# Giving GpSimd's work to VectorE and ScalarE, and keeping silu(cond) in DRAM, in a two-layer fp32 diffusion backbone

## The chip, the cores and the metric

The kernel runs on one core of a Trainium2 chip. The metric is the device time of one execution in microseconds (us), the median over runs. The core has five engines that matter here: TensorE (PE in the profile; PEld is its weight load), VectorE (DVE), ScalarE (ACT), GpSimd (POOL) and SyncE (SP), whose queue issues nearly all DMAs. Each engine works through its own instructions in order and waits on semaphores for the others.

## The reference

Two trunk layers over 512 latent and 128 context tokens of width 1024, all in fp32. The part that matters:

```python
def trunk_layer(x, cond, layer_idx, p, rope_mla, rope_diff, ctx):
    mod = jax.nn.silu(cond) @ p['ada_w'] + p['ada_b']
    shift, scale, gate = jnp.split(mod, 3, axis=-1)
    h = rmsnorm(x, p['norm_g']) * (1.0 + scale) + shift
    parts = jnp.split(h @ p['w_in'], _split_offsets(), axis=-1)
    c_q, c_kv, k_rope, cb, cc, cx, dq, dk, dv, z = parts
    ...
    o_mla, ckv, kr = mla_branch(c_q, c_kv, k_rope, p['q_norm'], p['w_uq'], p['kv_norm'], p['w_ukv'],
                                rope_mla, ctx_mla)
    o_conv = conv_branch(cb, cc, cx, p['conv_w'])
    ...
    o_diff, k_d, v_d = diff_branch(dq, dk, dv, p['lam'], p['subln'], lambda_init, rope_diff, ctx_diff)
    mix = jnp.concatenate([o_mla, o_conv, o_diff], axis=-1) * jax.nn.silu(z)
    x = x + gate * (mix @ p['w_out'])
    return x, (ckv, kr, k_d, v_d)
```

The latent attention (`mla_branch`) and the differential attention (`diff_branch`, two softmax maps a head) have four heads each; `k_rope` is rotated by `rope_mla` before it is used as a key. `cond` is one vector of 1024 for the latent tokens and one for the context tokens, so `mod` of a layer is 2 x 3072 numbers from a 1024 x 3072 matrix `ada_w`. A last RMSNorm closes the trunk. The outputs are both token groups and the new keys and values of each layer.

## The kernel before

x lies transposed in SBUF: 128 partitions, 8 blocks (`kt`) of the model width, 640 tokens. The tokens are worked on in two halves of 320 (`j` = 0, 1). Every fp32 product is done as three matmuls on split operands: `mm3` multiplies high by high (L362), high by low (L363) and low by high (L364). So every weight is loaded raw over the SP queue (L319), ScalarE casts it to its high part (`whi_...`, L324), and the low part `wli_... = raw - high` is one subtraction (L326) on the engine that the unit was given: GpSimd for the units qk2, cq1, c01, c11 of both layers and qk0, dv0 of layer 2, VectorE for the rest. A weight unit is 15 + 4 per layer, each in two halves of about 512 KB; the raw and split tiles come from a pool of 11 buffers with the tag "w".

The start: the condition vectors `cond` are loaded, silu is taken by ScalarE (L122, tanh) and VectorE (L123, L124) into `sc`, and 32 loads of 256 KB of the first layer's adaLN matrix (`ada`, L441) alternate on the SP queue with the loads of x (L416). Part 0 is summed by VectorE, parts 1 to 3 by TensorE (`pa`, L462), then moved and completed on VectorE (`mod`, L470, L161). Meanwhile the squares of x half 0 are taken by ScalarE (L236) and added up by GpSimd (L245), `st_n` and `rb_n` on TensorE turn the sum into a scale, VectorE forms `t` (L373), and `modulate` makes the high and low part of h: `hh` on ScalarE (L390), `hl` on VectorE (L394). The first projection `p0qk` runs over half 0 while GpSimd squares half 1 (L238, all eight issued at `kt` = 1 of that loop), VectorE adds them up, and the second half follows.

After that a generator `main()` emits all input projections of a layer, `units()` the attention units of both kinds (scores `S`/`Sm`, row maximum `sm`/`smm` on VectorE, exponential `E`/`Em` on ScalarE, transposes `tpd`/`tpm`, products `O`/`Om`), a list `bg` holds the work behind a projection (rotations, norms, weight splits), and `side()` computes the remaining adaLN vectors (the gate of layer 1 and all of layer 2) piece by piece on VectorE. `side()` needs silu(cond) broadcast over the partitions: `silu_bcast` loads 512 numbers of each of the two raw vectors to all partitions into the one buffer `cb` (L136), takes tanh on ScalarE into `tb` (L140, a tile of the "w" pool), and finishes silu with two VectorE instructions (L141, L142). It does so four times. Then for each piece `at` of 128 x 512 weights (L148, 256 KB) two multiply-and-sum instructions `jk` (L153) follow on VectorE. The rotary key of the latent attention is rotated by `rope` (L545, L547, L551 on GpSimd for `krf`, on VectorE for the other calls).

A scheduler of the tile framework sets the order of each engine's instructions from its own estimate of when they become ready, except where `pin` keeps program order (the first loads and casts, and the `cb` loads). So work given to another engine is placed anew, and the order around it shifts too.

Of the kernel before, what the change touches and what calls it, by code (L numbers as in the profile page):

```python
# [60 lines left out]
def tile_kernel(ctx: ExitStack, tc: tile.TileContext, i: dict, o: dict):  # L61
    nc = tc.nc
    V, S, G, TE = nc.vector, nc.scalar, nc.gpsimd, nc.tensor

# [8 lines left out]
    NBLK, NW = 37, 11  # L73
    PU = ("qk2", "cq1", "c01", "c11")
    QD, QM = 5, 3
# [48 lines left out]
    V.tensor_tensor(out=sc, in0=th0, in1=cond, op=ALU.mult)  # L124


    mod = [[cst.tile([P, KT, 2], F32, name="mod%d_%d" % (l, s)) for s in range(3)] for l in range(DEPTH)]
# [5 lines left out]

    def silu_bcast(hf, name):
        for c in range(2):
            pin(nc.sync.dma_start(out=cb2[:, c, :],  # L136
                                  in_=i["cond2"][c:c + 1, hf * 512:(hf + 1) * 512].broadcast_to([P, 512])))
        tb = wp.tile([P, 1024], F32, tag="w", name="tb" + name, bufs=NW, padded_shape=[P, 1088])
        tb = tb.rearrange("p (c n) -> p c n", c=2)
        S.activation(tb, cb2, AF.Tanh, scale=0.5)  # L140
        V.tensor_scalar(out=tb, in0=tb, scalar1=0.5, scalar2=0.5, op0=ALU.mult, op1=ALU.add)  # L141
        V.tensor_tensor(out=cb2, in0=cb2, in1=tb, op=ALU.mult)  # L142

# [80 lines left out]
    class Norm:  # L224


        def __init__(self, j, name, tag="blk", eng=V, sq=S):
            self.sq = sq
            self.j, self.name, self.sqs, self.tag, self.eng = j, "%s%d" % (name, j), [], tag, eng

        def add(self, x, kt):
            nm = "sq%s%d" % (self.name, kt)
            sq = slot(nm, shape=(P, HB)) if self.tag == "blk" else vtile(nm)[:, 0:HB]
            xj = x[:, self.j * HB:(self.j + 1) * HB]
            if self.sq is S:
                S.activation(sq, xj, AF.Square)  # L236
            else:
                self.sq.tensor_tensor(out=sq, in0=xj, in1=xj, op=ALU.mult)  # L238
            self.sqs.append(sq)
            while len(self.sqs) > (1 if kt == KT - 1 else 2):  # L240
                self.merge()

        def merge(self):
            a, b = self.sqs[0:2]
            self.eng.tensor_tensor(out=a, in0=a, in1=b, op=ALU.add)  # L245
            del self.sqs[1]
# [64 lines left out]

    def load_unit(src, w, name, tags, eng, res):

# [7 lines left out]
        for hf in range(2):  # L321
            hi = wtile_new(w, "wh%s%d" % (name, hf), tags[hf], F32R)
            lo = wtile_new(w, "wl%s%d" % (name, hf), tags[hf], F32R)
            pin(S.copy(hi, raws[hf]), len(loaded) < 4)  # L324
            yield
            eng.tensor_tensor(out=lo, in0=raws[hf], in1=hi.bitcast(F32), op=ALU.subtract)  # L326
            res.append((hi, lo))
            yield

    for l in range(DEPTH):  # L330
        for u in range(NU):
            src = i["wi"][l, :, :, 4 * UOFF[u]:4 * UOFF[u + 1]].rearrange("h p (k c) -> h p k c", k=4)
            unit_q.append((src, UW[u], "i%d_%s" % (l, UNITS[u]), ("w", "w"), G if l > 0 and u < 2 or UNITS[u] in PU else V))
        for u in range(4):
            unit_q.append((i["wo"][l, u].rearrange("h p (k c) -> h p k c", k=4), 256, "o%d_%d" % (l, u),
                           ("w", "w") if u < 3 else ("qs", "kh"), V))
    loaded = []
# [73 lines left out]
    x_dram = dr.tile([P, KT, T], F32, name="x_dram")  # L411
    norms = [Norm(0, "n0", "v", G), Norm(1, "n0", sq=G)]

# [97 lines left out]
    for l in range(DEPTH):  # L511
# [27 lines left out]

        def rope(dst, src, cos, sin, mask, name, rs=slice(0, P), eng=V):  # L540

            sh = slot("sh" + name, shape=(P, NL))
            V.stream_shuffle(sh[rs], lat(src)[rs], mask)
            yield
            eng.tensor_tensor(out=lat(dst)[rs], in0=lat(src)[rs], in1=cos[rs], op=ALU.mult)  # L545
            yield
            eng.tensor_tensor(out=sh[rs], in0=sh[rs], in1=sin[rs], op=ALU.mult)  # L547
            yield
            if eng is G:
                yield  # L550
            eng.tensor_tensor(out=lat(dst)[rs], in0=lat(dst)[rs], in1=sh[rs], op=ALU.add)  # L551
            yield
# [203 lines left out]
        def kv_post(krt, ck):  # L756
# [11 lines left out]
            S.activation(sq, ck, AF.Square)  # L768
            yield from rope(krf, kr, cosm, sinm, SWAP8, "kr%d" % l, rs, G)
            ckA = slot("ckA%d" % l)  # L770
# [190 lines left out]
        def main():  # L961
# [4 lines left out]
            for j in range(2):  # L966
                ps = [bank("p%dqk0%d%d" % (l, b, j))[:, 0:HB] for b in range(2)]
                js = slice(j * HB, (j + 1) * HB)
                for kt in range(KT):
# [12 lines left out]
                    if l == 0 and j == 0:  # L982
                        if kt == 1:
                            for k in range(KT):
                                norms[1].add(xs[k], k)
                        if kt == 6:
                            rg = norms[1].rstd()
# [38 lines left out]
        def side():  # L1026

            for step, (hf, parts) in enumerate((((0, ((l, 2),)), (1, ((l, 2), (l + 1, 0), (l + 1, 1))),
                                                 (0, ((l + 1, 0), (l + 1, 1))))) if l + 1 < DEPTH else
                                               ((0, ((l, 2),)), (1, ((l, 2),)))):  # L1030
                if step > 0 or l == 0:
                    silu_bcast(hf, "%d%d" % (l, step))
                for ll, s in parts:
# [194 lines left out]
def _layout(inp):  # L1228
# [6 lines left out]
    r["cond"] = np.stack([a["c"][0].reshape(P, KT), a["c_ctx"].reshape(P, KT)], axis=-1)  # L1235
    r["cond2"] = np.stack([a["c"][0], a["c_ctx"]])
    r["ident"] = np.concatenate([np.eye(P), np.zeros((P, 2))], axis=1).astype(np.float32)
# [84 lines left out]
```

## Time and profile before

| | |
|---|---|
| median of 3 runs (lowest, highest) | 825.05 us (823.18, 825.55) |
| the profiled execution: its time, its span | 825.69 us, 823.9 us |
| mean granted TensorE clock | 0.989 |
| busy: PE, PEld, DVE, ACT, POOL | 785.5, 741.3, 622.1, 449.9, 68.9 us |
| chain that ended last, shares | PE 70%, DVE 13%, DMA 7%, ACT 5%, issue 3%, POOL 1% |
| HBM read, written | 78.14 MB, 6.46 MB |

The span is the time from the first to the last instruction of the profiled execution; 1.8 us of its time lie outside it. Busy times say how full an engine is on the average; what ends a wait has to be read from the chain and the waits of one stretch. A granted clock of 1.00 is 2.4 GHz on TensorE, 0.50 is 1.2 GHz.

### The profile page before, as it was taken

The page shows a single profiled execution, that of the slowest core. Times are in us where ns is not written, and L with a number is a line of the kernel's source. Part 1 is how long each engine was busy: PE and PEld are TensorE (multiplying, and loading weights), DVE is VectorE, ACT ScalarE, POOL GpSimd, SP SyncE. Part 2 cuts the span into 40 slices and gives each one's busy share as a digit, 9 for nine tenths or more (in the row PEclk, how much of TensorE's full clock was granted, in tenths as well). Part 3 has the DMA queues.
Part 4 walks back from the last instruction along what each step waited for, and adds up shares of the span by engine and source line. Part 5 has one row for each costly group of instructions (what it writes and reads, how often), then busy time and mean ns, then how long its engine had stood idle before and what let it go on. Part 6 is the DMA issues. An engine that isn't in the chain of part 4 may idle for free.

```text
span 823.9 us, 14193 instructions
## 1 busy us (share of the span) xinstructions
PE 785.5 (95%) x5390; PEld 741.3 (90%) x5390; DVE 622.1 (76%) x1414; ACT 449.9 (55%) x978; POOL 68.9 (8%) x45
## 2 busy tenths in 40 slices
PE   6999998999999988999999999999999899999994
PEld 1389998999999988999999999999999899899994
DVE  4788998989897677779567478877788556668635
ACT  2255456556666566673334556565667567755310
POOL 3300020030002002000220001011000200200000
PEclk9999999999999999999999999999999999999997
DMA  8926424221421232135730322222212201221503
GB/s 309 386 74 187 144 69 158 75 88 57 146 84 39 55 132 88 46 122 188 246 103 27 100 82 68 64 64 71 93 39 77 65 26 65 64 91 43 189 1 127
DMA packets 66163, 85.51 MB, mean 104 GB/s; under 512 B 4976, under 2 KB 47408, under 8 KB 66096
## 3 DMA queue, kind: packets, MB, share of 16 engines
q1 hardware_dynamic: 65520, 83.96, 31.2%
q8 instruction: 42, 0.69, 0.3%
q10 hardware_dynamic: 576, 0.66, 0.2%
q14 instruction: 25, 0.20, 0.1%
HBM read 78.14 MB, written 6.46 MB: 103 GB/s over the span
## 4 chain that ended last, share of the span: by engine, by line
PE 70%; DVE 13%; DMA 7%; ACT 5%; issue 3%; POOL 1%; SPq 0%; POOLq 0%; DVEq 0%; ACTq 0%
PE wo L363 4%; PE wo L364 4%; PE wo L362 4%; PE O L651 3%; DVE jk L153 2%; PE v L362 2%; PE v L364 2%; PE v L363 2%; PE S L620 2%; PE p1qk L363 2%; PE p1qk L362 2%; PE tpm L905 2%; PE p1qk L364 2%; PE p1c L362 2%; PE p1c L363 2%
## 5 line engine op out<-in xcount | busy, mean ns | idle before, releaser
L153 DVE CUSTOM_DVE_ANT_0 jk<-at,cb 128x512 bf16<-128x512 f32 x128 | 89.6, 700 | 8.7 <-DMA at<-in_adaT 7.7
L637 ACT ACTIVATE E<-S,sm 128x640 f32<-128x640 f32 (+1 forms) x80 | 56.5, 709 | 45.5 <-DVE sm L631 41.7
L363 PE MATMUL wo<-mx,who 128*128 128x320 f32 x256 | 78.9, 311 | 0.5 <-DVE mx L274 0.2
L364 PE MATMUL wo<-mx,wlo 128*128 128x320 f32 x256 | 78.5, 309 | 0.0
L362 PE MATMUL wo<-mx,who 128*128 128x320 f32 x256 | 78.2, 311 | 0.0
L631 DVE TENSOR_REDUCE sm<-S 128x1 f32<-128x640 f32 (+1 forms) x80 | 55.0, 711 | 5.4 <-PE S L621 5.0
L236 ACT ACTIVATE sqn<-xn 128x320 f32<-128x320 f32 x32 | 14.9, 470 | 64.2 <-DVE xn L1170 57.5
L894 ACT ACTIVATE Em<-Sm,smm 128x640 f32<-128x640 f32 (+1 forms) x40 | 28.3, 708 | 39.0 <-DVE smm L892 37.7
L363 PEld LDWEIGHTS wo<-mx,who 128*128 128x128 f32 x256 | 48.0, 188 | 1.4 <-DVE mx L274 1.3
L364 PEld LDWEIGHTS wo<-mx,wlo 128*128 128x128 f32 x256 | 48.1, 188 | 0.0
L362 PEld LDWEIGHTS wo<-mx,who 128*128 128x128 f32 x256 | 47.7, 188 | 0.0
L362 PE MATMUL v<-whi_dv,hh 128*128 128x272 f32 x160 | 46.3, 290 | 0.0
L363 PE MATMUL v<-wli_dv,hh 128*128 128x272 f32 x160 | 46.0, 288 | 0.0
L364 PE MATMUL v<-whi_dv,hl 128*128 128x272 f32 x160 | 46.0, 288 | 0.0
L620 PE MATMUL S<-kh,qs 128*128 128x320 f32 x128 | 40.6, 327 | 5.4 <-ACT E L637 4.6
L651 PE MATMUL O<-v,atd 128*128 128x128 f32 x336 | 43.9, 274 | 0.0
L363 PE MATMUL p0qk<-hl,whi_qk 128*128 128x320 f32 x128 | 40.0, 313 | 2.4 <-DVE hl L394 2.4
L326 POOL TENSOR_TENSOR wli_c<-ri_c,whi_c 128x1024 fp32r<-128x1024 f32 x8 | 19.8, 2477 | 267.9 <-PE p1zm L363 84.9
L651 PEld LDWEIGHTS O<-v,atd 128*128 128x128 f32 x336 | 41.9, 191 | 0.0
L362 PE MATMUL p1c<-hh,whi_c 128*128 128x320 f32 x128 | 41.5, 325 | 0.0
L362 PE MATMUL p0c<-hh,whi_c 128*128 128x320 f32 x128 | 41.5, 324 | 0.0
L362 PE MATMUL p0qk<-hh,whi_qk 128*128 128x320 f32 x128 | 39.6, 320 | 1.4 <-ACT hh L390 1.4
(375 smaller groups left out, 2627.7 us busy)
## 6 DMA issues: line engine op xcount, KB each, us to landing
at<-in_adaT SPq DMA_DIRECT2D x64, 256.0 KB, 3.9
ada<-in_adaA SPq DMA_DIRECT2D x32, 256.0 KB, 5.1
ri_qk<-in_wi SPq DMA_DIRECT2D x16, 512.0 KB, 4.8
ri_c<-in_wi SPq DMA_DIRECT2D x16, 512.0 KB, 4.8
ro<-in_wo SPq DMA_DIRECT2D x16, 512.0 KB, 4.6
ri_dv<-in_wi SPq DMA_DIRECT2D x8, 544.0 KB, 4.9
ri_zd<-in_wi SPq DMA_DIRECT2D x8, 512.0 KB, 4.2
x<-in_xT SPq DMA_DIRECT2D x16, 160.0 KB, 5.0
```

The source lines that it names most:

```text
L153: V.tensor_tensor_reduce(out=junk, in0=raw, in1=cb2[:, c, :], scale=1.0, scalar=0.0, op0=ALU.mult, op1=ALU.add, accum_out=acc)
L236: S.activation(sq, xj, AF.Square)
L326: eng.tensor_tensor(out=lo, in0=raws[hf], in1=hi.bitcast(F32), op=ALU.subtract)
L362: TE.matmul(ps, ah, bh, start=first, stop=False)
L363: TE.matmul(ps, ah, bl, start=False, stop=False)
L364: TE.matmul(ps, al, bh, start=False, stop=last)
L620: TE.matmul(ps[:, j, 0:HB], qs[:, a, qc], kh[:, a, js], start=True, stop=False)
L631: V.tensor_reduce(out=sm[:, a:a + 1], in_=Sv[a], axis=AX.XY if u < 4 else AX.X, op=ALU.min)
L637: S.activation(ev, Sv[a], AF.Exp, bias=sm[:, a:a + 1], scale=-1.0, accum_out=so)
L651: TE.matmul(po[:, 0:128], at[:, c * 128:(c + 1) * 128], vv[:, h * 128:(h + 1) * 128], start=c == 0, stop=c == n - 1)
L894: S.activation(e if u < 4 else e[:, 0:128], Sv, AF.Exp, bias=sm[:, 0:1], scale=-1.0, accum_out=sm[:, 2:3])
L905: TE.transpose(tp[:, c * 128:(c + 1) * 128], toktile(e, c), ident)
```

## The change

GpSimd gets no instruction any more. All low parts of weights (L326), the rotation of `krf` and the sums of the first norm's half 0 are VectorE's; the squares of half 1 are ScalarE's, two each at `kt` = 2 to 5 of the first projection's loop, and the norm's statistics are started at `kt` = 7 of that loop and not at 6. silu(cond), which VectorE has in `sc`, is copied to a tile `scr`, stored to a DRAM tile `silu` over the SP queue, and `silu_bcast` becomes two broadcast loads from it: tanh, the two VectorE instructions and the tile `tb` are gone, as is the input `cond2`.

```diff
-    PU = ("qk2", "cq1", "c01", "c11")
...
     V.tensor_tensor(out=sc, in0=th0, in1=cond, op=ALU.mult)
 
+    scr = cst.tile([P, 2, KT], F32, name="scr")
+    V.tensor_copy(scr, sc.rearrange("p k c -> p c k"))
+    silu = dr.tile([2, D], F32, name="silu")
+    nc.sync.dma_start(out=silu.rearrange("c (p k) -> p c k", p=P), in_=scr)
...
-    def silu_bcast(hf, name):
+    def silu_bcast(hf):
         for c in range(2):
             pin(nc.sync.dma_start(out=cb2[:, c, :],
-                                  in_=i["cond2"][c:c + 1, hf * 512:(hf + 1) * 512].broadcast_to([P, 512])))
-        tb = wp.tile([P, 1024], F32, tag="w", name="tb" + name, bufs=NW, padded_shape=[P, 1088])
-        tb = tb.rearrange("p (c n) -> p c n", c=2)
-        S.activation(tb, cb2, AF.Tanh, scale=0.5)
-        V.tensor_scalar(out=tb, in0=tb, scalar1=0.5, scalar2=0.5, op0=ALU.mult, op1=ALU.add)
-        V.tensor_tensor(out=cb2, in0=cb2, in1=tb, op=ALU.mult)
+                                  in_=silu[c:c + 1, hf * 512:(hf + 1) * 512].broadcast_to([P, 512])))
...
-            if self.sq is S:
-                S.activation(sq, xj, AF.Square)
-            else:
-                self.sq.tensor_tensor(out=sq, in0=xj, in1=xj, op=ALU.mult)
+            S.activation(sq, xj, AF.Square)
...
         def merge(self):
             a, b = self.sqs[0:2]
-            self.eng.tensor_tensor(out=a, in0=a, in1=b, op=ALU.add)
+            V.tensor_tensor(out=a, in0=a, in1=b, op=ALU.add)
...
-            eng.tensor_tensor(out=lo, in0=raws[hf], in1=hi.bitcast(F32), op=ALU.subtract)
+            V.tensor_tensor(out=lo, in0=raws[hf], in1=hi.bitcast(F32), op=ALU.subtract)
...
-    norms = [Norm(0, "n0", "v", G), Norm(1, "n0", sq=G)]
+    norms = [Norm(0, "n0", "v"), Norm(1, "n0")]
...
-            eng.tensor_tensor(out=lat(dst)[rs], in0=lat(src)[rs], in1=cos[rs], op=ALU.mult)
+            V.tensor_tensor(out=lat(dst)[rs], in0=lat(src)[rs], in1=cos[rs], op=ALU.mult)
...
-            yield from rope(krf, kr, cosm, sinm, SWAP8, "kr%d" % l, rs, G)
+            yield from rope(krf, kr, cosm, sinm, SWAP8, "kr%d" % l, rs)
...
                     if l == 0 and j == 0:
-                        if kt == 1:
-                            for k in range(KT):
+                        if 2 <= kt < 6:
+                            for k in (2 * kt - 4, 2 * kt - 3):
                                 norms[1].add(xs[k], k)
-                        if kt == 6:
+                        if kt == KT - 1:
```

The order on the engines moves at three places that matter. First the SP queue at the start, before and after (`ada` are the adaLN loads, `scr` the tile with silu):

```order
L104 DMA small_in<-in_small 128x92
L441 DMA ada_0_135<-in_adaA 128x512
L441 DMA ada_1_137<-in_adaA 128x512
L441 DMA ada_0_139<-in_adaA 128x512
L416 DMA x_0_115<-in_xT 128x320
```

```order
L103 DMA small_in<-in_small 128x92
L128 DMA silu<-scr 128x2x8
L436 DMA ada_0_139<-in_adaA 128x512
L436 DMA ada_1_141<-in_adaA 128x512
L436 DMA ada_0_143<-in_adaA 128x512
L411 DMA x_0_119<-in_xT 128x320
```

The store of `silu` stands ahead of every load of `ada` and x, and it waits for VectorE's copy.

Second, VectorE where layer 1 goes from the first condition half to the second (the row maximum `sm_1_4` at the end is that of the attention unit which TensorE waits for there), before and after:

```order
L642 SCALAR_TENSOR_TENSOR E_0_3_1305<-E_0_3_1307,sm_0_3_1292,E_0_3_1305 128x640
L579 TENSOR_TENSOR klz_114<-kf_1_1254,hk_1_1340 64x640 x2
L141 TENSOR_SCALAR tb_1352<-tb_1352 128x1024
L142 TENSOR_TENSOR cb_109<-cb_109,tb_1352 128x1024
L695 SCALAR_TENSOR_TENSOR z0zd_1241<-z0zd_1241,p0zd_1332 128x320
L153 ISA jk_1358,mod_2_105<-at_1356,cb_109 128x512
L153 ISA mod_2_105 128x1
L631 TENSOR_REDUCE sm_1_4_1420<-S_1_4_1421 128x1
```

```order
L635 SCALAR_TENSOR_TENSOR E_0_3_1305<-E_0_3_1307,sm_0_3_1292,E_0_3_1305 128x640
L321 TENSOR_TENSOR wli_qk_1320<-ri_qk_1245,whi_qk_1319 128x4x256
L572 TENSOR_TENSOR klz_118<-kf_1_1254,hk_1_1340 64x640
L152 ISA jk_1354,mod_2_109<-at_1352,cb_113 128x512
L152 ISA mod_2_109 128x1
L688 SCALAR_TENSOR_TENSOR z0zd_1241<-z0zd_1241,p0zd_1332 128x320
L152 ISA jk_1356,mod_2_109<-at_1352,cb_113 128x512
L152 ISA mod_2_109 128x1
L572 TENSOR_TENSOR klz_118<-kf_1_1254,hk_1_1340 64x640
L152 ISA jk_1409,mod_2_109<-at_1407,cb_113 128x512
L152 ISA mod_2_109 128x1
L624 TENSOR_REDUCE sm_1_4_1416<-S_1_4_1417 128x1
```

The two instructions on `tb` and `cb` are gone; a low part of qk2 stands in front, and two more `jk` and one of the two `klz` come between E and the row maximum.

Third, VectorE in layer 2 ahead of the latent attention's values `vm` (`e`, `y_d`, `w_d` are steps of the differential heads' norm), before and after:

```order
L661 SCALAR_TENSOR_TENSOR e_3_7525<-s_3_6925 128x5
L896 RECIPROCAL smm_0_0_7486<-smm_0_0_7486 128x1
L663 SCALAR_TENSOR_TENSOR e_3_7525<-ss_3_6924,e_3_7525 128x5
L194 TENSOR_SCALAR y_d_3_7528<-e_3_7525 128x5
L197 TENSOR_TENSOR w_d_3_7529<-y_d_3_7528 128x5
...
L828 TENSOR_TENSOR vm_0_7545<-vm_0_7551,vm_0_7545 128x4x64
```

```order
L654 SCALAR_TENSOR_TENSOR e_3_7513<-s_3_6917 128x5
L321 TENSOR_TENSOR wli_c_7596<-ri_c_7585,whi_c_7595 128x4x256
L889 RECIPROCAL smm_0_0_7474<-smm_0_0_7474 128x1
L321 TENSOR_TENSOR wli_c_7640<-ri_c_7587,whi_c_7639 128x4x256
L656 SCALAR_TENSOR_TENSOR e_3_7513<-ss_3_6916,e_3_7513 128x5
L193 TENSOR_SCALAR y_d_3_7516<-e_3_7513 128x5
L196 TENSOR_TENSOR w_d_3_7517<-y_d_3_7516 128x5
...
L821 TENSOR_TENSOR vm_0_7533<-vm_0_7539,vm_0_7533 128x4x64
```

The two low parts of the unit c01 stand on VectorE now, ahead of `e` and with it of `vm`.

## Rows read from the trace of the kernel before

**Rows 1.** The page's busy times of the engines: us, share of the span, instructions.

```profile
PE 785.5 (95%) x5390; PEld 741.3 (90%) x5390; DVE 622.1 (76%) x1414; ACT 449.9 (55%) x978; POOL 68.9 (8%) x45
```

**Rows 2.** Busy time by stage: the stretch in us, its length, busy us (instructions) of PE, PEld, DVE, ACT and POOL, then the granted clock, the DMA share and GB/s.

```profile
0.00:37.70 37.70, 30.70 (x84) 7.20 (x84) 21.24 (x52) 9.21 (x17) 10.91 (x15) 1.00 0.96 343
37.70:62.00 24.30, 21.82 (x152) 20.39 (x153) 21.43 (x52) 13.86 (x29) 4.85 (x5) 1.00 0.33 120
62.00:140.00 78.00, 74.10 (x529) 72.15 (x528) 69.45 (x155) 44.16 (x103) 5.13 (x2) 0.98 0.44 137
140.00:260.00 120.00, 119.65 (x864) 117.16 (x862) 107.98 (x262) 74.78 (x180) 6.58 (x5) 1.00 0.28 89
260.00:345.00 85.00, 78.27 (x535) 74.02 (x534) 61.83 (x142) 54.91 (x111) 10.28 (x4) 1.00 0.25 75
```

**Rows 3.** The waits of TensorE: instruction and line, what it waited for, us in total, times, the longest.

```profile
PE S L620 <- ACT E L637: 4.6, 3, 2.6
PE Sm L362 <- ACT Em L894: 3.7, 4, 1.3
PE vm L823 <- DVE vm L828: 3.3, 2, 2.3
PE p0qk L363 <- DVE hl L394: 2.4, 4, 0.9
...
PE p0qk L362 <- ACT hh L390: 1.4, 2, 0.8
PE tpm L600 <- ACT Em L897: 1.3, 1, 1.3
```

**Rows 4.** GpSimd's instructions by line: shapes, count, busy us, mean ns of one, idle time before them.

```profile
L326 POOL TENSOR_TENSOR wli_c<-ri_c,whi_c 128x1024 fp32r<-128x1024 f32 x8 | 19.8, 2477 | 267.9 <-PE p1zm L363 84.9 <-PE p0zm L363 84.1 <-PE p0c L363 49.8
L326 POOL TENSOR_TENSOR wli_qk<-ri_qk,whi_qk 128x1024 fp32r<-128x1024 f32 x6 | 15.1, 2510 | 207.0 <-PE wo L363 75.4 <-PE p1qk L363 67.8 <-PE p0qk L363 63.6
L238 POOL TENSOR_TENSOR sqn<-x 128x320 f32<-128x320 f32 x8 | 8.5, 1096 | 13.4 <-DMA x<-in_xT 13.4
L245 POOL TENSOR_TENSOR sqn<-sqn,sqn 128x320 f32<-128x320 f32 x7 | 7.1, 1007 | 13.2 <-ACT sqn L236 12.8
L326 POOL TENSOR_TENSOR wli_cq<-ri_cq,whi_cq 128x512 fp32r<-128x512 f32 x4 | 5.2, 1292 | 6.5 <-issue 6.2 <-ACT whi_cq L324 0.2
L326 POOL TENSOR_TENSOR wli_dv<-ri_dv,whi_dv 128x1088 fp32r<-128x1088 f32 x2 | 5.1, 2554 | 17.0 <-PE wo L363 17.0
...
L545 POOL TENSOR_TENSOR krf<-kr,cosm 32x512 f32<-32x512 f32 x2 | 2.6, 1284 | 110.5 <-ACT kr L764 110.5
```

**Rows 5.** VectorE's instructions of the same kinds, and one of the removed ones, by line and shape, with the same columns.

```profile
L326 DVE TENSOR_TENSOR wli_qk<-ri_qk,whi_qk 128x1024 fp32r<-128x1024 f32 x10 | 12.5, 1246 | 1.7 <-ACT whi_qk L324 1.6
...
L326 DVE TENSOR_TENSOR wli_c<-ri_c,whi_c 128x1024 fp32r<-128x1024 f32 x8 | 9.7, 1215 | 0.3 <-ACT Em L894 0.2
...
L551 DVE TENSOR_TENSOR kf<-kf,shk 128x512 f32<-128x512 f32 x8 | 5.5, 685 | 0.1
...
L142 DVE TENSOR_TENSOR cb<-cb,tb 128x1024 f32<-128x1024 f32 x4 | 4.9, 1224 | 0.1
```

**Rows 6.** Five VectorE groups by the tile that they write: count, then the shortest, the median and the longest duration of one in ns, the first and last start in us, and the shapes.

```profile
L153 DVE CUSTOM_DVE_ANT_0 jk<-at,cb x128: 671/683/2783, 79.2 to 753.4; 128x512 bf16<-128x512 f32 x128
L562 DVE TENSOR_TENSOR qs<-raw0qk,qs x8: 685/686/2432, 72.8 to 200.4; 64x512 fp32r<-64x512 f32 x8
L245 DVE TENSOR_TENSOR sqn<-sqn,sqn x35: 478/492/2507, 41.9 to 811.7; 128x320 f32<-128x320 f32 x35
L394 DVE SCALAR_TENSOR_TENSOR hl<-t,mod,hh x48: 342/410/1004, 38.2 to 451.2; 128x320 fp32r<-128x320 f32 x16, 128x192 fp32r<-128x192 f32 x16, 128x128 fp32r<-128x128 f32 x16
L197 DVE TENSOR_TENSOR w_d<-y_d x8: 156/165/2194, 139.2 to 648.9; 128x5 f32<-128x5 f32 x8
```

**Rows 7.** The start by the timeline, start us and duration us first: SP's issue of the first three `ada` loads.

```profile
2.12 1.38 SPq L441 DMA_DIRECT2D ada<-in_adaA  x3
```

**Rows 8.** VectorE's timeline in the same stretch: the instruction that completes silu(cond).

```profile
3.98 0.17 DVE L124 TENSOR_TENSOR sc<-th,cond 128x16 f32<-128x16 f32 x1
```

**Rows 9.** The chain of waits from 117 to 131 us: start us, duration us, what.

```profile
119.06 3.84 DMA cb<-in_cond
...
122.98 1.07 ACT tb L140
...
124.07 0.70 DVE tb L141
```

**Rows 10.** The chain of waits from 640 to 655 us, with the same columns.

```profile
646.32 1.05 ACT whi_c L324
...
648.93 2.21 DVE w_d L197
...
651.73 0.34 DVE vm L828
```

**Rows 11.** Busy times as in the second group, of the stretch after the stalls at 126 and at 650 us.

```profile
129.80:133.10 3.30, 3.30 (x12) 2.90 (x12) 2.15 (x6) 1.80 (x4) 0.00 (x0) 0.50 0.02 5
...
652.10:655.30 3.20, 3.18 (x8) 2.65 (x9) 2.33 (x8) 0.97 (x3) 0.00 (x0) 0.50 0.53 164
```

**Rows 12.** The chain of waits from 280 to 300 us, with the columns of the ninth group.

```profile
284.20 4.77 DMA cb<-in_cond
...
289.07 1.06 ACT tb L140
```

More of the change, by code (lines that the diff above doesn't have):

```diff
@@ L62, in tile_kernel @@
     nc = tc.nc
-    V, S, G, TE = nc.vector, nc.scalar, nc.gpsimd, nc.tensor
+    V, S, TE = nc.vector, nc.scalar, nc.tensor
     cst = ctx.enter_context(tc.tile_pool(name="cst", bufs=1))
@@ L224, in tile_kernel, with __init__ @@
     class Norm:
-        def __init__(self, j, name, tag="blk", eng=V, sq=S):
-            self.sq = sq
-            self.j, self.name, self.sqs, self.tag, self.eng = j, "%s%d" % (name, j), [], tag, eng
+        def __init__(self, j, name, tag="blk"):
+            self.j, self.name, self.sqs, self.tag = j, "%s%d" % (name, j), [], tag
         def add(self, x, kt):
@@ L310, in tile_kernel, with load_unit @@
     unit_q = []
-    def load_unit(src, w, name, tags, eng, res):
+    def load_unit(src, w, name, tags, res):
         raws = []
@@ L332, in tile_kernel @@
             src = i["wi"][l, :, :, 4 * UOFF[u]:4 * UOFF[u + 1]].rearrange("h p (k c) -> h p k c", k=4)
-            unit_q.append((src, UW[u], "i%d_%s" % (l, UNITS[u]), ("w", "w"), G if l > 0 and u < 2 or UNITS[u] in PU else V))
+            unit_q.append((src, UW[u], "i%d_%s" % (l, UNITS[u]), ("w", "w")))
         for u in range(4):
             unit_q.append((i["wo"][l, u].rearrange("h p (k c) -> h p k c", k=4), 256, "o%d_%d" % (l, u),
-                           ("w", "w") if u < 3 else ("qs", "kh"), V))
+                           ("w", "w") if u < 3 else ("qs", "kh")))
     loaded = []
@@ L538, in proj_raw, with rope @@
             return r
-        def rope(dst, src, cos, sin, mask, name, rs=slice(0, P), eng=V):
+        def rope(dst, src, cos, sin, mask, name, rs=slice(0, P)):
             sh = slot("sh" + name, shape=(P, NL))
@@ L544, in rope @@
             yield
-            eng.tensor_tensor(out=lat(dst)[rs], in0=lat(src)[rs], in1=cos[rs], op=ALU.mult)
+            V.tensor_tensor(out=lat(dst)[rs], in0=lat(src)[rs], in1=cos[rs], op=ALU.mult)
             yield
-            eng.tensor_tensor(out=sh[rs], in0=sh[rs], in1=sin[rs], op=ALU.mult)
+            V.tensor_tensor(out=sh[rs], in0=sh[rs], in1=sin[rs], op=ALU.mult)
             yield
-            if eng is G:
-                yield
-            eng.tensor_tensor(out=lat(dst)[rs], in0=lat(dst)[rs], in1=sh[rs], op=ALU.add)
+            V.tensor_tensor(out=lat(dst)[rs], in0=lat(dst)[rs], in1=sh[rs], op=ALU.add)
             yield
@@ L1031, in side @@
                 if step > 0 or l == 0:
-                    silu_bcast(hf, "%d%d" % (l, step))
+                    silu_bcast(hf)
                 for ll, s in parts:
@@ L1235, in _layout @@
     r["cond"] = np.stack([a["c"][0].reshape(P, KT), a["c_ctx"].reshape(P, KT)], axis=-1)
-    r["cond2"] = np.stack([a["c"][0], a["c_ctx"]])
     r["ident"] = np.concatenate([np.eye(P), np.zeros((P, 2))], axis=1).astype(np.float32)
```

## The prediction

> **What bounds the kernel now.** I read the busy times first. TensorE is busy 785.5 us [rows 1], so at most some 38 us of a span of 823.9 us are to be had or lost by waits, and most changes on other engines stay hidden until TensorE waits for them. The busy times by stage show where that can be: from 140 to 260 us TensorE works 119.65 of 120 us, so a gain there is worth nothing and only a loss can show; from 62 to 140 us it lacks 3.9 us, from 260 to 345 us 6.7 us, and up to 62 us it lacks 9.5 us [rows 2]. The reader sees there too that VectorE is the second engine: 69.45 of 78 us and 107.98 of 120 us, 90% between 62 and 260 us, and that the DMA engines are taken 0.96 of the first 37.7 us. The waits of TensorE then name the releasers: exponentials (S, Sm), values vm, the low and high parts of h [rows 3]. The chains around 126 and 650 us, the two longest of these waits, come last [rows 9, 10].
>
> **VectorE's balance.** It takes over 8 wli_c at 1.215 us, 6 wli_qk at 1.246 and 2 wli_dv at about 1.3 (an estimate, wli_qk by width), 4 wli_cq at about 0.65 (half as wide), 6 rotation steps of 0.685 and 7 sums of 0.492: 9.7 + 7.5 + 2.6 + 2.6 + 4.1 + 3.4 = 29.9 us [rows 4, 5, 6]. It loses four times 0.70 and 1.224, 7.7 us [rows 5, 9]. Against the remaining 22 us stands something that the tile rows show: single instructions of VectorE take 2.0 to 2.5 us more or less at once, and it is the same kind that otherwise takes a small fraction of it: a jk 2.78 for 0.683, a qs 2.43 for 0.686, a sqn 2.51 for 0.492, a w_d of five numbers a partition 2.19 for 0.165 [rows 6]. The excess is 1.75 to 2.1 us, near the 2.5 us that a low part takes on GpSimd [rows 4], and the times of the latter (646 to 651 us for the last) fit. With 16 long GpSimd parts, one such excess for half of them to all of them is 16 to 32 us. I take 22, so VectorE's total stays about where it is; the bounds are 0 (then +22 us on VectorE) and all of GpSimd's 68.9 us. ScalarE gets 8 squares of about 0.5 us (nearest row: VectorE's 0.492 of the same shape) and loses four tanh of 1.07: 3.9 against 4.3 us, no change [rows 6, 9].
>
> The Trainium skill's page "SBUF — State Buffer" (Who interferes with whom) says that VectorE instructions with two SBUF inputs contend with GpSimd instructions that read SBUF, and that the one issued second blocks until the first is finished. The tile rows agree in kind. By that rule each overlap would cost up to the remaining length of the GpSimd instruction, which would put the relief nearer to the upper figure of 32 us; the sum here does not use it.
>
> **The start.** The store of silu stands on the SP queue ahead of every ada and x load. The first ada was issued at 2.12 us [rows 7]; silu is ready at 3.98 + 0.17 = 4.15 [rows 8], the copy takes another 0.17, a step of the queue 0.46 (1.38 / 3) and the hand-over about 0.13, so ada starts at 4.9, 2.8 us later. Behind it are 32 ada and 16 x loads with the DMA engines 0.96 busy, so nothing hides it: +2.8 up to where the first projection starts. What comes back: GpSimd's squares of half 1 (8.5 us) run beside the low parts of h, which then take up to 1.0 us where the median is 0.41, and TensorE waits 2.4 us for them and 1.4 us for hh [rows 3, 4, 6]. VectorE is busy 21.43 of 24.30 us in that stage [rows 2]. Now ScalarE puts eight squares between the hh. I take back a third of the 3.8 us, 1.2 (between 0 and 2.8). Sum +1.6, from 0 to +2.8. The sums of half 0 cost 3.4 us on a VectorE that is busy 21 of 37.7 us: hidden.
>
> **The wait at 126 us.** The chain is: last jk of the first half, load of cb 3.84 us, tanh 1.07, VectorE 0.70 and 1.22, then jk and row maxima, then the exponential [rows 5, 9]. The load stays, the other 3.0 us go. But the order shows what steps in between E and the same row maximum: a low part of qk2 (1.25) and two more jk (2 x 0.68); the jk now waits for cb, with z0zd, the second klz and the row maximum queued behind it. 3.0 - 2.6 = 0.4. Upstream two qs were among the long ones, about 2.4 us together beyond their median, against 1.25 for the first low part of qk2: another 1.1. I take -1.5 (from -2.6 to 0). After this stall TensorE's granted clock is 0.50 for 3.30 us, after the stall at 650 for 3.20 us, that is 1.2 in place of 2.4 GHz, worth half: 1.6 each [rows 11]. Stalls of up to 1.3 us from 260 to 345 us left the clock at 1.00 [rows 2, 3], so a shorter stall should keep it: -1.6.
>
> **The wait at 650 us.** vm waits behind w_d, which took 2.21 us in place of 0.165, under a low part on GpSimd [rows 6, 10]. That goes, -2.05. The low parts of c01 now stand ahead of e on VectorE. The second needs its cast, which ends at 646.32 + 1.05 = 647.37, so it ends near 648.6; e started about 0.3 us ahead of y_d and w_d at 648.4, so 0.2 us is lost, and a little for what the first one delays: -1.7 (from -2.05 to 0), and its clock -1.6.
>
> **Other waits.** The one transposition that waited 1.3 us for Em [rows 3] stood behind the jk of 2.78 us [rows 6]: -1.0. Between 260 and 345 us one load of cb takes 4.77 us and tanh starts at 289.07 [rows 12]; tanh and two products, 3.0 us, go from that path, and tb gives its weight buffer back; four low parts of c (4.9 us) come to a VectorE with 23 us free [rows 2, 5]. TensorE lacks 6.7 us there; I take -1.8 (from -4 to 0).
>
> **What the returned work costs.** In layer 1 it comes at 168 to 180 us, where VectorE is 90% busy: three steps of the rotation and two wli_cq, 3.4 us, and the same in layer 2, 6.7 us in all. On TensorE's path this is 0 if VectorE's free 12 us [rows 2] take it, 6.7 if nothing does; GpSimd's 1.3 us parts there slowed VectorE too. A quarter: +1.6. The low parts of the layer change (398 to 425 us) and of layer 2's qk2 lie beside a TensorE that lacks nothing: 0, and 2.5 each if the cover is gone.
>
> **Sum.** +1.6 - 1.5 - 1.6 - 1.7 - 1.6 - 1.0 - 1.8 + 1.6 = -6.0. The profiled execution took 825.69 us, so 819.7; that execution is 0.64 above the median of 825.05, so 819.0 on the median's footing, between 816 and 822.5.
>
> **Rivals.**
> The gains are swallowed. The start costs its full 2.8, the wait at 126 us keeps all but 0.4 of itself and so its slow clock, 650 us gives 1.7 + 1.6, the other waits give 1.0 and the returned work costs 1.6: 2.8 - 0.4 - 3.3 - 1.0 + 1.6 = -0.3, 824.8. For it speaks the order at 126 us, where as much steps in as goes; against it, that GpSimd's shadow is seen in so many groups.
> VectorE becomes the bound, slower. Between 62 and 260 us it is at 90%; it takes two low parts of qk2 (2.5) and 3.4 us of rotation and wli_cq there, and if the long instructions were not GpSimd's doing nothing comes back. Place: 106 to 180 us. From less than about 2.5 us of relief there it decides, since TensorE then waits for row maxima all along. Price 5.9 + 2.8 at the start - 3.3 at 650 us = +5.4: 830.4. Against it: from 140 to 260 us TensorE lacks 0.35 us though VectorE was already slowed there.
> The Trainium skill's page "Perfetto Trace Analysis" (Optimizing Scalar/DVE Operations) has the rule behind this rival: where VectorE is saturated, moving work from it to ScalarE or even GpSimd may make sense. It says in the same place that GpSimd and VectorE share a read port, so that shifting between these two might not help, which the tile rows bear out.
> A fuller gain. The start costs nothing on balance, the wait at 126 us goes with 2.6 + 1.6, 650 with 2.05 + 1.6, the transposition with 1.3, 260 to 345 us with 4, the returned work is hidden: -13.2, 811.9. For it: each of these is the end of a bound worked out above; against it, that all of them would have to come true.
>
> **How the numbers follow.** My forecast 0.47, the gains swallowed 0.22, VectorE the bound 0.19, the fuller gain 0.12. The range from 812 to 829 leaves out the lowest part of the last and the upper half of the slower case. A measurement of this kernel can tell about 0.3%, 2.5 us, from no change. Faster: 0.47 + 0.12 and 0.01 of the swallowed case, 0.60; same 0.21; slower 0.19.
>
> **What would show it.** In the profile of the changed kernel: no POOL instruction, jk, qs, w_d and hl with their longest near their median; VectorE's total near 622 us (640 and more speaks for the slower case); the first ada issued near 4.9 us and the first projection at about 39 to 40.5 against 37.8; vm near 650 us with a wait under 0.5 us, the wait at 126 us near 1 us, and no stretch of clock 0.50 before the tail. The forecast is wrong if TensorE lacks more than 2 us between 140 and 260 us, if the long VectorE instructions stay, or if the start's 2.8 us are still there at 62 us.

## The result, and the profile after

The changed kernel takes 813.23 us (median of 6 runs, 811.61 to 815.65) where the kernel before takes 823.89 us (6 runs, 821.77 to 825.55): a ratio of 0.9874, 95% interval 0.9852 to 0.9897, or 10.7 us less. The forecast was 6.0 us less. The profiled execution took 812.95 us, 12.7 us less than the profiled one before, which lay 1.8 us above its median.

The busy times by engine and then by stage answer to [rows 1] and [rows 2] (same columns; since the changed program is ahead by up to 12 us, the same stretch of time holds a little later work).

```profile
PE 781.6 (96%) x5390; PEld 738.0 (91%) x5390; DVE 615.3 (76%) x1440; ACT 449.3 (55%) x982; POOL 0.2 (0%) x4
```

```profile
0.00:37.70 37.70, 31.43 (x82) 7.11 (x83) 21.49 (x58) 8.63 (x15) 0.20 (x4) 1.00 0.90 319
37.70:62.00 24.30, 21.97 (x149) 19.76 (x148) 19.45 (x52) 16.70 (x36) 0.00 (x0) 1.00 0.43 154
62.00:140.00 78.00, 75.77 (x557) 74.53 (x556) 68.46 (x165) 45.62 (x111) 0.00 (x0) 1.00 0.46 147
140.00:260.00 120.00, 117.10 (x839) 113.92 (x838) 106.30 (x257) 72.02 (x172) 0.00 (x0) 1.00 0.27 82
260.00:345.00 85.00, 83.34 (x580) 79.98 (x579) 64.43 (x153) 57.49 (x118) 0.00 (x0) 1.00 0.28 85
```

VectorE got 26 instructions more and is busy 6.8 us less. TensorE lacks 1.7 us between 260 and 345 us where it lacked 6.7, but 2.9 us between 140 and 260 us where it lacked 0.35. TensorE's waits (as [rows 3]) say the same: S is down to 2.9 us, Sm to 1.3 and vm (on VectorE) to 0.2. rb_k is new, between 170 and 180 us and near 556, and st_n, which waited once for VectorE before (1.9 us), has a second wait, of 1.2 us at 411 us.

```profile
PE st_n L211 <- DVE sqn L240: 3.1, 2, 1.9
PE p0qk L358 <- DVE hl L389: 3.0, 5, 0.9
PE S L613 <- ACT E L630: 2.9, 3, 1.5
...
PE rb_k L742 <- DVE y_k L202: 1.5, 2, 0.8
PE Sm L357 <- ACT Em L887: 1.3, 4, 0.5
...
PE vm L816 <- DVE vm L821: 0.2, 1, 0.2
```

The tile rows (as [rows 6]) have lost every long instruction: the longest jk is 0.694 us where it was 2.783.

```profile
L152 DVE CUSTOM_DVE_ANT_0 jk<-at,cb x128: 671/683/694, 77.1 to 741.1; 128x512 bf16<-128x512 f32 x128
...
L555 DVE TENSOR_TENSOR qs<-raw0qk,qs x8: 685/686/691, 73.5 to 199.4; 64x512 fp32r<-64x512 f32 x8
...
L240 DVE TENSOR_TENSOR sqn<-sqn,sqn x42: 480/492/494, 13.9 to 799.4; 128x320 f32<-128x320 f32 x42
...
L196 DVE TENSOR_TENSOR w_d<-y_d x8: 160/166/168, 136.4 to 642.2; 128x5 f32<-128x5 f32 x8
```

Where the time went follows from comparing the start of each matmul with that of the same one (same name, same place in its row) before, and taking the median difference over 10 us:

| stretch of the trace before, us | change in it, us | forecast |
|---|---|---|
| start, up to 62 | +0.7 | +1.6 |
| the wait at 126 with its clock | -3.8 | -3.1 |
| 170 to 225 | +3.4 | +1.6, with layer 2 |
| 262 to 340 | -6.1 | -1.8 |
| 355 to 380 | -1.1 | 0 |
| 411 to 440 | +1.0 | 0 |
| 510 | -1.5 | 0 |
| 555 to 575 | +1.2 | (in the 1.6) |
| 600 | -0.9 | 0 |
| 650 with its clock | -3.6 | -3.3 |
| 704 | -1.9 | -1.0 |
| the tail | -0.5 | 0 |

Together -13.1 us in this one pair of executions, as much as their spans differ (823.9 and 810.8 us). In the changed one the granted clock stays at 1.00 until the tail.

### The profile page after: what moved, and what is told of

Its sections match the earlier page's. It is cut to its first block, busy times and chain, and to the rows that moved or that the text cites. A ratio compares the mean times of both kernels' runs of the same rounds, so it can differ in the third digit from the quotient of the medians.

```text
span 810.8 us, 14105 instructions
## 1 busy us (share of the span) xinstructions
PE 781.6 (96%) x5390; PEld 738.0 (91%) x5390; DVE 615.3 (76%) x1440; ACT 449.3 (55%) x982; POOL 0.2 (0%) x4
## 4 chain that ended last, share of the span: by engine, by line
PE 46%; DVE 7%; ACT 2%; DMA 2%; issue 1%; SPq 0%; DVEq 0%; ACTq 0%
PE wo L358 4%; PE wo L359 4%; PE wo L357 4%; PE p1qk L358 2%; PE p1qk L357 2%; PE p1qk L359 2%; PE O L644 2%; PE p1c L359 2%; PE p1c L358 2%; PE p1c L357 2%; PE v L358 1%; PE v L359 1%; PE v L357 1%; PE S L613 1%; PE p1zd L357 1%; PE p1zd L359 1%
## 5 line engine op out<-in xcount | busy, mean ns | idle before, releaser
L152 DVE CUSTOM_DVE_ANT_0 jk<-at,cb 128x512 bf16<-128x512 f32 x128 | 87.6, 684 | 10.5 <-DMA at<-in_adaT 9.5
L357 PE MATMUL p1qk<-hh,whi_qk 128*128 128x320 f32 x128 | 40.4, 317 | 0.0
L1163 DVE SCALAR_TENSOR_TENSOR xn<-wo,mod,xn 128x320 f32<-128x320 f32 (+2 forms) x48 | 19.5, 434 | 27.2 <-PE wo L359 20.4
```

The source lines that it names most:

```text
L152: V.tensor_tensor_reduce(out=junk, in0=raw, in1=cb2[:, c, :], scale=1.0, scalar=0.0, op0=ALU.mult, op1=ALU.add, accum_out=acc)
L357: TE.matmul(ps, ah, bh, start=first, stop=False)
L1163: V.scalar_tensor_tensor(out=xn[kt][:, a:e], in0=ps[:, a - j * HB:e - j * HB], scalar=mod[l][2][:, kt, c:c + 1], in1=xn[kt][:, a:e], op0=A ...
```

## The experiments

Theory A: what the kernel before lost was VectorE's time under GpSimd's instructions, and, as lo_only narrows it, under the 20 low parts. Theory B: it was the chain of silu and the weight buffer that the chain held. Each ratio is to the kernel before, timed beside that run.

| run | median, us | ratio | interval |
|---|---|---|---|
| silu_only | 825.67 | 1.0026 | 1.0003 to 1.0050 |
| pool_only | 812.50 | 0.9859 | 0.9831 to 0.9887 |
| store_act | 811.82 | 0.9844 | 0.9821 to 0.9868 |
| shadow | 824.92 | 1.0012 | 0.9994 to 1.0029 |
| lo_only | 809.10 | 0.9805 | 0.9785 to 0.9824 |
| shadow_copy | 818.09 | 0.9921 | 0.9902 to 0.9940 |
| act_rope | 807.68 | 0.9786 | 0.9768 to 0.9804 |
| act_u2 | 810.86 | 0.9836 | 0.9813 to 0.9858 |
| lo_rope | 811.56 | 0.9850 | 0.9830 to 0.9869 |
| lo_norm | 809.11 | 0.9809 | 0.9786 to 0.9832 |
| lo_silu | 808.46 | 0.9815 | 0.9786 to 0.9843 |
| act_rope_u2 | 805.87 | 0.9782 | 0.9762 to 0.9802 |

**The two halves of the change apart.** silu_only is the kernel before with these lines of the change and no other:

```diff
+    nc.sync.dma_start(out=silu.rearrange("c (p k) -> p c k", p=P), in_=scr)
...
-                                  in_=i["cond2"][c:c + 1, hf * 512:(hf + 1) * 512].broadcast_to([P, 512])))
...
-        S.activation(tb, cb2, AF.Tanh, scale=0.5)
+                                  in_=silu[c:c + 1, hf * 512:(hf + 1) * 512].broadcast_to([P, 512])))
```

> The kernel before with only the silu part of the change: silu stored to DRAM at the start and broadcast from there; GpSimd keeps all its work. Theory A (most of the 10.7 us comes from VectorE no longer being slowed under GpSimd's instructions): 2 to 4 us faster than before, w_d still about 2.2 us long and vm still late near 650 us. Theory B (most comes from the silu chain and the weight buffer that it took): 7 to 10 us faster, with the stalls between 262 and 330 us gone.

pool_only takes the same lines back out of the changed kernel.

> The changed kernel with the old silu_bcast (load of the raw conditioning, tanh, two VectorE instructions, tile from the weight pool) and without the store at the start; GpSimd stays unused. Theory A: 6 to 9 us faster than before, the stall at 650 us gone, that at 126 us back. Theory B: 0 to 3 us faster, the stalls between 262 and 330 us back.

The silu part alone gains nothing, it is 0.26% slower; without it the rest of the change has the whole gain, 1.4%. Theory B is out. Theory A's sizes missed too: 2 to 4 us faster was expected of silu_only, and 6 to 9 of pool_only, which gains 11.6. silu_only's first 62 us are 2.4 us longer, the wait at 126 us gives 2.8 back, and near 317 us two VectorE instructions, kml, lie under a pair of GpSimd's low parts and take 5.16 us together. First its GpSimd timeline there, then VectorE's:

```profile
315.43 5.30 POOL L326 TENSOR_TENSOR wli_c<-ri_c,whi_c 128x1024 fp32r<-128x1024 f32 x2 [48.21 <-PE p0c L363]
```

```profile
316.25 5.16 DVE L861 TENSOR_TENSOR kml<-krf,kmh 32x640 fp32r<-32x640 f32 x2
```

In the kernel before, one of the two fell under it (1.98 us), the other had begun ahead of it (0.82). So TensorE's wait grew to 3.5 us there, and a small shift of the work upstream cost 3.9 us: what a GpSimd instruction costs depends on what happens to be under it.

**GpSimd's instructions put back, without their use.** shadow is the changed kernel, in which VectorE makes all low parts, with a subtraction of a weight's high part from itself on GpSimd into an unused tile.

```diff
+            if name[3:] in ("qk2", "cq1", "c01", "c11") or name in ("i1_qk0", "i1_dv0"):
+                jg = slot("jg%s%d" % (name, hf)).bitcast(BF16)[:, 0:4 * w].rearrange("p (k c) -> p k c", k=4)
+                G.tensor_tensor(out=jg, in0=hi.bitcast(F32), in1=hi.bitcast(F32), op=ALU.subtract)
             V.tensor_tensor(out=lo, in0=raws[hf], in1=hi.bitcast(F32), op=ALU.subtract)
```

> The changed kernel with GpSimd given a subtraction of the same size, of a weight's high part from itself into an unused tile, wherever it made a low part before (20 instructions); VectorE still makes the low parts. Theory A: VectorE's instructions of 2 us and more are back (w_d, jk, qs) and the kernel is 4 to 8 us slower than the changed one. Rival (VectorE was slow there for another reason, or it does not matter): within 1 us of the changed kernel.

All of the gain is gone: 824.92 us, 11.4 us above the changed kernel by the ratios, more than the 4 to 8 expected. Nothing uses what these instructions write (their tile only takes one of 37 buffers for a while), and TensorE never waits for them; one ScalarE instruction does, for 0.6 us. So their presence is what costs. Part of the price is TensorE's clock behind longer waits: the mean granted clock is 0.98 from 62 to 140 us and 0.99 from 140 to 260 us, where the changed kernel has 1.00. The tile rows show long instructions again, on sm and jk among others, while w_d and qs, which I had also named, stay at their medians. TensorE waits for up to 3.6 us for S and 2.3 us for rb_k, where the changed kernel has 1.5 and 0.8:

```profile
L636 DVE SCALAR_TENSOR_TENSOR sm<-s,sm,neglam x40: 201/219/1849, 92.7 to 643.9; 128x1 f32<-128x1 f32 x40
...
L152 DVE CUSTOM_DVE_ANT_0 jk<-at,cb x128: 669/685/2341, 76.8 to 752.7; 128x512 bf16<-128x512 f32 x128
```

```profile
PE S L616 <- ACT E L633: 5.5, 4, 3.6
...
PE rb_k L745 <- DVE y_k L202: 3.8, 2, 2.3
```

shadow_copy has a copy of the same tile there, one operand read in place of two:

```diff
-                G.tensor_tensor(out=jg, in0=hi.bitcast(F32), in1=hi.bitcast(F32), op=ALU.subtract)
+                G.tensor_copy(jg, hi.bitcast(F32))
```

> The changed kernel with GpSimd copying each of the 20 weights' high parts into an unused tile (one operand read) in place of subtracting it from itself (two operands read, run 'shadow'). If GpSimd's reading of two operands, or the length of its instruction, is what holds VectorE up, the copy costs half or less of the 11.7 us that the subtraction cost, 0 to 6 us above the changed kernel; if any GpSimd instruction that reads SBUF holds it up for its length, about 8 to 12 us above, with VectorE instructions near the copy's length.

It costs 0.5% against the changed kernel, some 4 us, a third of what the subtraction costs. The traces agree: counting VectorE's instructions that take over 0.25 us more than the median of their group, shadow has 9, which are 10.3 us over in all, shadow_copy 6 with 3.6 us, the changed kernel none, and the kernel before 24 with 25.9 us, of which 5.2 are left in lo_only below. GpSimd's groups in the two runs, first shadow, then shadow_copy:

```profile
L323 POOL TENSOR_TENSOR jgi_c<-whi_c 128x1024 bf16<-128x1024 f32 x8 | 16.9, 2110 | 285.8 <-PE Om L911 193.1 <-DVE smm L892 42.8 <-DVE mod L152 39.4
```

```profile
L323 POOL CAST jgi_c<-whi_c 128x1024 bf16<-128x1024 f32 x8 | 10.0, 1251 | 289.3 <-PE Om L911 192.4 <-DVE smm L892 43.5 <-DVE mod L152 40.4
```

The copy is 0.6 as long. Whether the rest is the one operand less was not separated. What the added instructions do to the order is not the cause of the difference: VectorE, ScalarE and TensorE have all their instructions in the same order in these two runs, so the 7.5 us between them come from GpSimd's instructions alone. Against the changed kernel 25 of VectorE's 1440 stand elsewhere, so a part of the remaining 4 us can be the order.

**The parts of the GpSimd half.** lo_only is the kernel before with one change:

```diff
-            unit_q.append((src, UW[u], "i%d_%s" % (l, UNITS[u]), ("w", "w"), G if l > 0 and u < 2 or UNITS[u] in PU else V))
+            unit_q.append((src, UW[u], "i%d_%s" % (l, UNITS[u]), ("w", "w"), V))
```

> The kernel before with one part of the change: all low parts of weights on VectorE. GpSimd keeps the squares and sums of the first norm and the rotation of krf; silu_bcast is the old one. If the 20 low parts are what GpSimd cost (theory A, narrowed), 9 to 12 us faster than before, as much as with GpSimd unused altogether; if norms and rotation share in it, 4 to 8 us.

1.95% faster, 16 us: more than the 9 to 12 expected, and more than the whole change. So something else in the change loses. lo_rope adds the rotation on VectorE:

```diff
-            yield from rope(krf, kr, cosm, sinm, SWAP8, "kr%d" % l, rs, G)
+            yield from rope(krf, kr, cosm, sinm, SWAP8, "kr%d" % l, rs)
```

> lo_only (the kernel before with all low parts on VectorE) and the rotation of krf on VectorE as well; norms and silu as before. Theory: the rotation's three instructions a layer stand in front of the kv norm on a VectorE that is 90% busy, and cost 3 to 5 us against lo_only (from the waits at 177, 189, 216 and 556 us). Rival: they are free there as VectorE has room, and the loss between 177 and 220 us comes from the low parts of cq1: within 1 us of lo_only.

It loses 0.45%, 3.7 us. The stage from 140 to 260 us, lo_only and then lo_rope, shows where. The third row, from lo_rope's waits of TensorE, shows on what: the norm's rb_k for 0.8 us at 177 us (and for 0.6 in layer 2), to which two waits of S at 187 and 215 us add 0.65:

```profile
140.00:260.00 120.00, 120.00 (x867) 117.76 (x866) 107.57 (x261) 73.65 (x177) 3.98 (x3) 1.00 0.27 81
```

```profile
140.00:260.00 120.00, 118.48 (x848) 115.47 (x848) 107.06 (x262) 72.43 (x174) 0.00 (x0) 1.00 0.27 82
```

```profile
PE rb_k L749 <- DVE y_k L203: 1.4, 2, 0.8
```

With all low parts on VectorE, those of cq1 among them, TensorE is busy without a gap; with the rotation there too it is not. lo_norm adds the norm's part of the change to lo_only:

> lo_only and the first norm's squares of half 1 on ScalarE and sums of half 0 on VectorE, as in the changed kernel; rotation and silu as before. Theory: what the eight squares between the hh cost and what GpSimd's shadow on hl cost balance, within 1 us of lo_only. Rival: GpSimd's shadow weighed more, 1 to 2 us faster.

No difference can be seen (0.9809 against 0.9805), though the intervals do not shut out the rival's 1 to 2 us. lo_silu adds the silu part, its store on ScalarE's queue:

> lo_only and the silu part, with its store on ScalarE's queue; norms and rotation stay on GpSimd. Theory: with the low parts gone from GpSimd the silu chain has little left to give (pool_only, without the silu part, is level with the changed kernel): 0 to 2 us faster than lo_only, at the wait at 126 us. Rival: the silu part is worth its 3 us of chain at 126 and at 289 us each: 3 to 6 us faster.

No difference either (0.9815): the rival, 3 to 6 us, is out.

**The store at the start, and a better version.** store_act is the changed kernel with one word different:

```diff
-    nc.sync.dma_start(out=silu.rearrange("c (p k) -> p c k", p=P), in_=scr)
+    nc.scalar.dma_start(out=silu.rearrange("c (p k) -> p c k", p=P), in_=scr)
```

> The changed kernel with the store of silu issued on ScalarE's queue and not on SP's, so that the adaLN loads no longer wait for it. If the store still costs its 0.7 us at the first projections' end (where the two profiles differ by that), the kernel is 0.7 us faster than the changed one; if what bounds the start is the data and not the issue, no difference (within 0.5 us); the first ada load is issued at 2.1 us either way.

It is 0.3% faster than the changed kernel by the ratios, 2.5 us, more than either expectation, though the intervals just overlap, so that the gain isn't certain. SP's first loads, in the changed kernel and then in store_act:

```profile
4.26 0.39 SPq L128 DMA_DIRECT2D silu<-scr  x1
4.69 1.42 SPq L436 DMA_DIRECT2D ada<-in_adaA  x3
```

```profile
2.11 1.38 SPq L436 DMA_DIRECT2D ada<-in_adaA  x3
```

Single profiles don't settle how much of this reaches 62 us: the five runs with this store stand there from -1.2 to +4.5 us against the kernel before. act_rope also gives the rotation of krf back to GpSimd:

> The changed kernel with the silu store on ScalarE's queue (as in store_act) and the rotation of krf back on GpSimd. Theory: the waits near 177 and 556 us (TensorE for rb_k, 0.8 and 0.6 us) come from the rotation standing on VectorE; with it on GpSimd they go and the kernel is 1 to 2 us faster than store_act, since three instructions of 32 partitions shadow little. Rival: they come from the low parts of cq1 on VectorE, or GpSimd's shadow costs as much again: 0 to 1 us slower than store_act.

0.9786 against store_act's 0.9844, some 4.8 us, more than expected; the loss between 170 and 225 us is gone (2.4 us in store_act's profile, 0.6 in this one). act_u2 gives back the four low parts of layer 2's first two units instead:

```diff
+        eng = G if name in ("i1_qk0", "i1_dv0") else V
...
-            V.tensor_tensor(out=lo, in0=raws[hf], in1=hi.bitcast(F32), op=ALU.subtract)
+            eng.tensor_tensor(out=lo, in0=raws[hf], in1=hi.bitcast(F32), op=ALU.subtract)
```

> The changed kernel with the silu store on ScalarE's queue (as in store_act) and the four low parts of layer 2's first two weight units (398 to 425 us) back on GpSimd. Theory: the wait of 1.2 us for the norm's sums at 411 us comes from those low parts standing ahead of the sums on VectorE; it goes, and the kernel is about 1 us faster than store_act. Rival: GpSimd's shadow on the sums costs as much: no difference or slower.

The wait for st_n at 411 us is gone in its profile, worth 1.4 us there; the time, 0.9836, can't be told from store_act's. But the reason that I gave was wrong. In the changed kernel VectorE has no low part before the norm's last sums; it has xn, which waits 2.95 us for the wo group that TensorE is just finishing. VectorE there, in the changed kernel:

```profile
410.96 0.68 DVE L1163 SCALAR_TENSOR_TENSOR xn<-wo,mod,xn 128x192 f32<-128x192 f32 x2 [2.95 <-PE wo L359]
411.56 1.11 DVE L240 TENSOR_TENSOR sqn<-sqn,sqn 128x320 f32<-128x320 f32 x2
```

So st_n waits for sums that stand behind an eviction of TensorE's last group: an order that the scheduler made, and made otherwise when four low parts went elsewhere. act_rope_u2 has both:

> The changed kernel with the silu store on ScalarE's queue, the rotation of krf and the four low parts of layer 2's first two units back on GpSimd. If the two gains add, 0.7 us faster than act_rope, near 807 us where before is 825; if the low parts on GpSimd delay the first projection of layer 2, no faster than act_rope.

At 805.87 us, 0.9782, it has the lowest time of the study, 2.2% below the kernel before and 0.9% below the changed one. Against act_rope the second step can't be told from nothing, and the interval overlaps that of lo_only, which changes one line of the kernel before: that what it has beyond lo_only gains anything is not shown.

## Why the prediction was right or wrong

**VectorE's balance: right.** Forecast near 622 us, measured 615.3 against 622.1; the relief pays for all returned work and a little more. The long instructions, whose excess I had put at 22 us, were 25.9 us over their medians in the kernel before and are gone.

**Direction and place: right; size: too small.** The forecast was 819.0 us, between 816 and 822.5, and 812 to 829 with the rivals; 813.23 lies below the first of these and inside the second, and the gain is 10.7 us and not 6.0. The step that failed is the term "Other waits", above all the -1.8 for 260 to 345 us. Measured: -6.1 there, beyond its bound of -4, -1.9 and not -1.0 for the transposition, and -3.5 at 355 to 380, 510 and 600 us, where I had counted nothing; lo_only's trace has these three too (-1.1, -1.5, -0.7). In all -11.5 where I had -2.8. I had seen the relief only as VectorE's balance, and put a price only on waits whose chain I had followed. Between 260 and 345 us two steps of the differential heads' norm, e, were long ahead of vm, for which TensorE waited 1.05 us; VectorE before, then in the changed kernel:

```profile
263.06 2.17 DVE L661 SCALAR_TENSOR_TENSOR e<-s 128x5 f32<-128x5 f32 x1
...
266.46 1.22 DVE L663 SCALAR_TENSOR_TENSOR e<-ss,e 128x5 f32<-128x5 f32 x1 [1.15 <-ACT jk L654]
```

```profile
263.81 0.15 DVE L654 SCALAR_TENSOR_TENSOR e<-s 128x5 f32<-128x5 f32 x1
...
266.92 0.16 DVE L656 SCALAR_TENSOR_TENSOR e<-ss,e 128x5 f32<-128x5 f32 x1
```

A kml of 1.98 us stood ahead of the wait for Em at 322 us. For the rest the way is not shown. A qs of 2.85 and an sm of 2.03 us stand at 493 to 498 us, 15 us ahead of the wait at 513, with idle time of VectorE in between. And no GpSimd instruction runs from 268 to 317, from 323 to 398 or from 561 to 646 us, yet the waits at 290, 304 and 601 us shrink and 355 to 380 us gets shorter when the low parts leave GpSimd. Most of that term I also credited to the wrong half of the change: tanh and its two products (3.0 us on that path). lo_only and lo_silu show that the low parts account for it, and that the silu chain gives nothing once they are off GpSimd. lo_only's own trace goes from -4.8 to -11.1 us between 260 and 340 us with the old silu chain still in; TensorE lacks 1.5 us there:

```profile
260.00:345.00 85.00, 83.53 (x578) 79.74 (x577) 67.07 (x157) 59.02 (x116) 0.00 (x0) 1.00 0.32 96
```

That the total came as near as it did is partly luck: the 8.7 us missed here are in part made up by 4.0 us of cost that I missed below.

**The wait at 650 us: right; at 126 us: right in size, not in its main reason.** -3.6 and -3.8 against -3.3 and -3.1. At 650 us the low parts do stand ahead of e, the second right in front of it; w_d is 0.17 us again and TensorE waits 0.2 us for vm (VectorE, the changed kernel; the time is 6.8 us earlier; [rows 10]):

```profile
640.66 1.23 DVE L321 TENSOR_TENSOR wli_c<-ri_c,whi_c 128x1024 fp32r<-128x1024 f32 x1
641.81 0.16 DVE L656 SCALAR_TENSOR_TENSOR e<-ss,e 128x5 f32<-128x5 f32 x1
...
642.21 0.17 DVE L196 TENSOR_TENSOR w_d<-y_d 128x5 f32<-128x5 f32 x1
...
642.68 0.42 DVE L821 TENSOR_TENSOR vm<-vm,vm 128x256 fp32r<-128x256 f32 x1
```

At 126 us the wait is 1.5 us where I said about 1, and the clock stays at 1.00 behind it ([rows 11] had 0.50):

```profile
128.00:131.50 3.50, 3.50 (x24) 3.48 (x25) 3.11 (x8) 2.73 (x8) 0.00 (x0) 1.00 0.02 5
```

Either half of the change shortens this wait: in the profile of silu_only the same stretch gives 2.8 us, in that of pool_only 1.5. But lo_only, which keeps tanh and its products, gives 4.2, so the 3.0 us of chain that my sum started from did not have to go. What does go there is the excess of the two long qs, which was 1.75 and 1.22 us, 3.0 in all, and not the 2.4 that I read.

**What the returned work costs: too small.** +1.6 forecast, +3.4 in layer 1 and +1.2 in layer 2 measured, and +1.0 at the layer change, where I had 0. TensorE lacks 2.9 us between 140 and 260 us, over the 2 us that I had named as a sign of being wrong. "A quarter of 6.7" took VectorE's free 12 us between 140 and 260 us as cover; two thirds came through. Free time on the average did not help, because the rotation stands in front of the kv norm and of row maxima on an engine that is 90% busy. The profile of lo_rope points to the rotation rather than to cq1's low parts, and the gain of act_rope agrees.

**The start: issue time right, its price open.** The first ada was issued at 4.69 us (forecast 4.9; the store was issued 0.03 us after the copy, where I had put 0.13 for the hand-over). But the first projection starts at 38.73 us against 37.78, 0.95 later and not 2.8 (in silu_only's profile, with the same store, 2.4 later). At 62 us 0.7 are left in the changed kernel's profile, where I said 1.6; the start varies by more than that from run to run, so the size stays open. Of TensorE's 3.8 us of waits for hl and hh, of which I took 1.2 back, 3.0 are left, all for hl. The norm's part shows no effect on the time by itself (lo_norm), though its one profile is 1.6 us ahead of lo_only's at 62 us.

**The rivals.** VectorE did not become the bound, and the gains were not swallowed. The fuller gain (811.9) came nearest in its total, but not by its terms: its returned work was not hidden, and part of its gain lies at waits that it did not name.

## What to carry to other kernels

A small engine's busy share says nothing about what it costs: GpSimd was busy 8%, and its 20 low parts cost 16 us. Look for single instructions far above their group's median on the engine beside it, and charge them to every path they can stand on, not only to the waits that a chain happens to show. When work is taken back, move it part by part: here the long, wide subtractions had to go, while three short ones before a norm were better left where they were.

## What was not expected of the hardware

Under GpSimd's instructions only some of VectorE's are slowed. In the trace of the kernel before, the tile rows of the softmax (shortest, median and longest in ns) separate them:

```profile
L631 DVE TENSOR_REDUCE sm<-S x80: 278/816/826, 90.9 to 636.2; 128x1 f32<-128x640 f32 x64, 128x1 f32<-128x128 f32 x16
L639 DVE RECIPROCAL sm<-sm x40: 142/162/167, 92.5 to 639.5; 128x1 f32<-128x1 f32 x40
L640 DVE SCALAR_TENSOR_TENSOR sm<-s,sm,neglam x40: 201/219/2027, 92.7 to 639.7; 128x1 f32<-128x1 f32 x40
...
L910 DVE TENSOR_TENSOR plm<-tpm,phm x32: 805/823/826, 275.5 to 748.0; 128x640 fp32r<-128x640 f32 x32
```

The reduction reads PSUM, the reciprocal one SBUF operand, plm one of each: of these 7, 5 and 2 overlap a GpSimd instruction in time and none is longer than usual. L640 takes its operands from SBUF: 4 overlap, 3 are held, for a single number per partition. That is how a w_d of five numbers a partition could take 2.2 us.

The Trainium skill's page "SBUF — State Buffer" (Who interferes with whom) says that a VectorE instruction with two inputs in SBUF contends with a GpSimd instruction that reads SBUF, and that one with at most one input there, outside the modes that use two ports, does not. These rows agree. The 20 subtractions whose result nothing uses show what it cost here: 11.4 us. By the Trainium skill's page "Perfetto Trace Analysis" (Optimizing Scalar/DVE Operations) shifting work between GpSimd and VectorE might not help; here taking the low parts back gained 16 us, and taking the rotation back lost 3.7.
